# Score rows in paired PSUM banks, and input squares summed on VectorE, in a one-core hybrid decoder layer

## The chip, the core and the metric

The kernel runs on one core of a Trainium2 chip. TensorE (PE) multiplies matrices from SBUF into PSUM, which has eight banks of 512 fp32 columns on 128 partitions. VectorE (DVE) and ScalarE (ACT) read PSUM and SBUF, GpSimd (POOL) works on SBUF, and SyncE (SP) issues the DMAs. The metric is device time in microseconds (us); less is better.

## The reference, cut to what matters

One decoder layer over 1024 tokens of width 1024, all in fp32:

```python
u = rmsnorm(h, g_mix)                       # mean of squares over the 1024 features of a token
z = u @ w_in                                # 1440 columns: x_rnn, x_gate, c_q, c_kv, k_rope
y_rnn = rglru_group(x_rnn, x_gate, ...)     # causal conv, two gates, linear recurrence, gelu
q  = rmsnorm(c_q) @ w_q_up; kv = rmsnorm(c_kv) @ w_kv_up     # 8 heads, 96 columns of q and k
s  = (q . k) * scale, causal                # blocks of 128 queries
p  = softmax(s)                             # row maximum, exponential, row sum
y_att = p @ v
h = h + concat(rmsnorm(y_rnn), rmsnorm(y_att)) @ w_out
h = h + (silu(v @ w_gate) * (v @ w_up)) @ w_down             # v = rmsnorm(h); 2816 wide
h = h + sigmoid(rmsnorm(h) @ w_ple_gate) * rmsnorm(p_in @ w_ple_proj)
return rmsnorm(h, g_final)
```

## The kernel before

The layout is transposed: features on partitions, the 1024 tokens along the free dimension. Each fp32 operand is split into a high and a low part on ACT (`x_h`) and DVE (`x_l`), so that one product is three matmuls (high-high, high-low, low-high) of 128 x 128 by 512 columns.

No instruction is issued where the program text calls it. The calls are recorded, and `Plan.order` lays them out by a list scheduler: each engine takes, of the operations whose inputs are ready by the plan's own estimates, the one with the smallest key. The key is the operation's number in program order, plus an offset for some tiles (`OFF`). An operation whose output tile is in a pool (`bank`: the eight PSUM banks; `slot`: 51 SBUF tiles) can start only when the pool has a free one, and for banks one stays reserved while any bank called for earlier in program order has not been given out (`RES`). The engines then run their lists in that fixed order, and semaphores guard every dependency. Line 361 is the one line that issues everything, so every row below says L361 and is known by its tile names.

The stages that matter here:

- **Input.** For each of eight blocks `k` of the input, `xr` and a weight `w` (`w1`) arrive by DMA, are split, and PE runs 12 matmuls into four banks (`g1`: c_kv and k_rope, shown as `g_a`, `g_b`). `sq_acc` squares the block on ACT, and POOL adds it to `x_acc`. From `x_acc` the `rstd` steps make 1/rms: PE transposes (`nx_ms`), DVE sums (`n_ss`), ACT takes the root (`n_rt`), DVE refines (`n_r`, `n_t`), PE transposes back (`nx_bc`), ACT copies to `nx_rb`. Meanwhile PE runs `in_mm(0)` and `in_mm(1)` (tiles `wn_a`, `wn_b`, 48 matmuls each). `evac` multiplies each bank by its half of `nx_rb` on DVE, and that frees it. DVE also builds the rotary angles (`ang`, `turns`) in this time.
- **Projections and recurrence.** Eight more `in_mm` tiles, with the recurrence on ACT, DVE and POOL.
- **Attention.** For each of 8 heads and 8 query blocks `qb`, `scores` multiplies into one bank (up to 512 keys) or two (`qb` 4 to 7), takes a negated maximum per bank (`nm`), where there are two banks the smaller of the two (a 128 x 1 operation), then one exponential per bank with its row sum read out. `tav_steps` transposes the blocks (`tp`), splits them (`pt`, in part over `pf` on POOL) and multiplies by v (`av`).
- **Output projection, FFN, gate.** FFN products take three banks each (`ff_z`, `ff_y`, `ff_x`); a bank is read by DVE or ACT after each block of matmuls (12 matmuls for gate and up, 6 to 9 for down), and `ff_z` goes on accumulating after it was read.

Of the kernel before, what the change touches and what calls it, by code (L numbers as in the profile page):

```python
# [122 lines left out]
class Buf:  # L123
    def __init__(self, pool, shape, dt, name, tag, bufs):
        self.args, self.tag, self.cap, self.name = (pool, shape, dt), tag, bufs, name
        self.real, self.log, self.left, self.placed = None, [], 0, False


class Op:
# [12 lines left out]
class Plan:  # L142


    def __init__(self, nc):
        self.nc, self.ops, self.tags, self.hold = nc, [], {}, None
        self.engines = {n: getattr(nc, n) for n in ("vector", "scalar", "gpsimd", "tensor", "sync")}

    def tile(self, pool, shape, dt, name, tag, bufs):
# [18 lines left out]
    def cost(self, eng, fn, a, k, out):  # L168
        w = out.width() if isinstance(out, View) else 0
        if fn == "dma_start":  # L170
            v = k["out"] if isinstance(k["out"], View) else k["in_"]
            return v.shape[0] * v.width() * 4 / 360e3, 2.1
        if eng == "tensor":
            if fn == "transpose":
                return 0.108, 0.18
            return w * 0.000417 + 0.0135, 0.18
        if eng == "vector":
            if fn == "reciprocal":
                return 0.065 + w * 0.0063, 0.13
            if fn in ("tensor_reduce", "reduce_sum"):  # L180
                return 0.065 + k["in_"].width() * 0.00104, 0.13
            ptr = 0.061 * any(isinstance(x, View) for x in (k.get("scalar"), *a[2:])) if fn == "scalar_tensor_tensor" else 0.0
            one = fn in ("tensor_copy", "tensor_scalar", "tensor_scalar_mul", "tensor_scalar_add", "tensor_scalar_max")
            if one and all(v.buf.tag != "bank" for v in [*a, *k.values()] if isinstance(v, View)):
                return 0.068 + w * 0.00052, 0.13
            return 0.068 + ptr + w * 0.00104, 0.13
        if eng == "scalar":
            src = k["in_"] if "in_" in k else a[1]
            c = (0.052 if src.buf.tag == "bank" else 0.093) + w * 0.000833
            c += 0.093 * sum(isinstance(k.get(n), View) for n in ("scale", "bias", "accum_out"))  # L190
            return c, 0.14
        return 0.15 + w * (0.0033 if fn == "tensor_copy" else 0.0022), 0.14

# [9 lines left out]
    def add(self, eng, fn, a, k):  # L203
        o = Op()
        o.eng, o.fn, o.a, o.k, o.idx = eng, fn, a, k, len(self.ops)
        o.succ, o.npred, o.ready = [], 0, 0.0
        out = k["out"] if "out" in k else a[0]
        outs = [v for v in (out, k.get("accum_out")) if isinstance(v, View)]
        rest = list(a[1:] if "out" not in k else a) + [v for n, v in k.items() if n not in ("out", "accum_out")]
        ins = [v for v in rest if isinstance(v, View)]  # L210
        o.cost, o.lat = self.cost(eng, fn, a, k, out)
        o.port = self.shares(eng, fn, [v for v in ins if v.width() > 8])
        f = k.get("func") or next((x for x in a if isinstance(x, AF)), None)
        o.table = f.name if eng == "scalar" and f is not None and f.name in FIRST else None
        preds = {self.hold: True} if self.hold else {}
        for v, w in [(v, False) for v in ins] + [(v, True) for v in outs]:
            p0, p1, c0, c1 = v.region
            keep = []
            for (q, r, qw) in v.buf.log:
                hit = r[0] < p1 and p0 < r[1] and r[2] < c1 and c0 < r[3]  # L220
                if hit and (w or qw) and q is not o:
                    preds[q] = True
                if not (w and q is not o and p0 <= r[0] and r[1] <= p1 and c0 <= r[2] and r[3] <= c1):
                    keep.append((q, r, qw))
            keep.append((o, v.region, w))
            v.buf.log = keep
        o.key = o.idx + OFF.get(eng[0] + out.buf.name.rstrip('_ab') if isinstance(out, View) else '', 0) + (DEF if eng in ('vector', 'scalar') and not any(v.buf.tag == 'bank' for v in ins + outs) else 0)
        o.bufs = list(dict.fromkeys(v.buf for v in ins + outs))
        for b in o.bufs:
            if not b.left:  # L230
                b.first = o.idx
            b.left += 1
        for q in preds:
            q.succ.append(o)
            o.npred += 1
        self.ops.append(o)
        return o

    def order(self):
# [14 lines left out]
        table = ""  # L254
        port = 0.0
        frees = []
        for o in self.ops:
            if not o.npred:
                heapq.heappush(avail[o.eng], (o.key, o.idx, o))
# [7 lines left out]

        while left:
            while frees and frees[0][0] <= t:
                _, _, tag, n = heapq.heappop(frees)  # L270
                free[tag] += n
            moved = False
            for e in names:
                while future[e] and future[e][0][0] <= t:
# [6 lines left out]
                while avail[e] and tries < 40:  # L281
                    i, _, o = heapq.heappop(avail[e])
                    tries += 1
                    ok = all(b.placed or free[b.tag] > min(unplaced(b), RES.get(b.tag, 99)) for b in o.bufs)
                    if ok:
                        key = i
                        if e == "scalar" and o.table and o.table not in SAME.get(table, ()):
# [25 lines left out]
                for b in o.bufs:  # L313
                    if b.placed:
                        continue
                    b.placed = True
                    free[b.tag] -= 1
                    q, d = queue[b.tag], ahead[b.tag]
                    d[b.pos] = True
                    while head[b.tag] < len(q) and d[head[b.tag]]:  # L320
# [6 lines left out]
                for b in o.bufs:  # L327
                    b.left -= 1
                    b.done = max(getattr(b, "done", 0.0), o.end)
                    if not b.left:  # L330
                        heapq.heappush(frees, (b.done, b.pos, b.tag, 1))
                for s in o.succ:
                    s.npred -= 1
                    r = start + c + (LAT[e, s.eng] if (e, s.eng) in LAT else o.lat)
# [17 lines left out]
    def emit(self):  # L352
        for o in self.order():
            for b in o.bufs:
                if b.real is not None:
                    continue
                pool, shape, dt = b.args
                b.real = pool.tile(shape, dt, name=b.name, tag=b.tag, bufs=b.cap)
            a = [x.real() if isinstance(x, View) else x for x in o.a]
            k = {n: x.real() if isinstance(x, View) else x for n, x in o.k.items()}  # L360
# [4 lines left out]
DEF = 0  # L365
FG = ((0, 1), (2, 3), (4, 5), (6, 7))
TK = 5
VA = ()
VS = ()
X0 = 0  # L370
SWITCH = 150
RES = {'bank': 1, 'slot': 99}
# [3 lines left out]
def hybrid_layer(ctx, tc, xT, pT, pos, vec, const, const2, w1, wn, wrg, wq, wkv, wo, wg, wu, *rest):  # L376
# [18 lines left out]

    def bank(name):
        return plan.tile(psp, [P, HB], F32, name, "bank", 8)

    def small(shape, name, bufs=2, dt=F32):
        return plan.tile(sml, shape, dt, name, name, bufs)  # L400
# [104 lines left out]

    INVF, ALPHA, BETA, GAMMA = (ccol(i) for i in range(4))

    def sq_acc(acc, src, first, eng, dve=False):
        t = acc if first else slot("sq")
        if dve:  # L510
            V.tensor_mul(t, src, src)
        else:
            A.activation(t, src, AF.Square)
        if not first:
            eng.tensor_add(acc, acc, t)

# [98 lines left out]
        tabs.extend((sc, cse, cpos, cneg))  # L615


    g1 = [pair("g1") for _ in range(2)]
    acc = slot("x_acc")
    xs = []  # L620
    for k in range(8):
# [22 lines left out]
            tb = tables()  # L644
            next(tb)
        xs.append(x2)
        sq_acc(acc, xr, k == 0, V if k in VA else G, k in VS)
        for i in range(2):
            c = slice(i * P, (i + 1) * P)
            mm(g1[i], wh[:, c], wl[:, c], x2, k == 0, k == 7)  # L650
# [6 lines left out]

    def in_mm(i, mid=None):
        wh, wl = weight(("wn", i), 2 if i < 9 else 0)
        pss = pair("wn")  # L660
        for k in range(8):
            c = slice(k * P, (k + 1) * P)
            mm(pss, wh[:, c], wl[:, c], xs[k], k == 0, k == 7)
            if mid and k == 3:
                mid()
        return pss

    def evac(pss, dst):
        for h in range(2):
            V.tensor_mul(dst[:, HS[h]], pss[h], rxs[0][:, HS[h]])  # L670

    cq0p = in_mm(0, lambda: next(nx))

# [5 lines left out]


    ckv = slot("ckv")
    evac(g1[0], ckv)
    krz = slot("krz")
    evac(g1[1], krz)
    cq = [slot("cq0"), slot("cq1")]
    evac(cq0p, cq[0])
    evac(in_mm(1), cq[1])
# [174 lines left out]
    def scores(hd, qb):  # L862
        if qb == 0:
            pA, pA3 = slot("pA"), slot("pA3")
            st[hd] = {"p": {0: pA[:, 0:128], 1: pA[:, 128:384], 2: pA[:, 384:768], 3: pA3[:, 0:512]},
                      "rs": small([P, 2, 8], "rs"), "nm": small([P, 8, 2], "nm")}
        if qb >= 4:
            st[hd]["p"][qb] = slot("pB")
        pd, rs, nm = st[hd]["p"][qb], st[hd]["rs"], st[hd]["nm"]
        (qh, ql), (kh, kl) = qs[hd], ks[hd]  # L870
        n = (qb + 1) * P
        cc = slice(qb * P, (qb + 1) * P)
        chunks = [(c0, min(c0 + HB, n)) for c0 in range(0, n, HB)]
        pss = []
        for i, (c0, c1) in enumerate(chunks):
            w = c1 - c0
            ps = bank("s")
            pss.append(ps)
            T.matmul(ps[:, :w], lhsT=qh[:, cc], rhs=kh[:, c0:c1], start=True, stop=False)
            T.matmul(ps[:, :w], lhsT=qh[:, cc], rhs=kl[:, c0:c1], start=False, stop=False)  # L880
            if c1 == n:
                T.matmul(ps[:, w - P:w], lhsT=ib, rhs=mb, start=False, stop=False)
            T.matmul(ps[:, :w], lhsT=ql[:, cc], rhs=kh[:, c0:c1], start=False, stop=True)
            V.tensor_reduce(out=nm[:, qb, i:i + 1], in_=ps[:, :w], axis=AX.X, op=ALU.max, negate=True)
        if len(chunks) == 2:
            V.tensor_tensor(out=nm[:, qb, 0:1], in0=nm[:, qb, 0:1], in1=nm[:, qb, 1:2], op=ALU.min)
        for i, (c0, c1) in enumerate(chunks):
            A.activation(pd[:, c0:c1], pss[i][:, :c1 - c0], AF.Exp, bias=nm[:, qb, 0:1], accum_out=rs[:, i, qb:qb + 1])

    def tav_steps(hd, hf):  # L890
        q0, nk = 4 * hf, 4 * hf + 4
# [28 lines left out]
        def fin():  # L920
# [6 lines left out]
            V.tensor_add(dst[main, HS[hf]], av[0][main], dst[main, HS[hf]])  # L927
            if hf:
                rs = st[hd]["rs"]
                V.tensor_add(rs[:, 0, 4:8], rs[:, 0, 4:8], rs[:, 1, 4:8])  # L930
                V.reciprocal(ris[-1][:, :, 1 - hd % 2], rs[:, 0])

        def go(i):
            if i < nk:
# [557 lines left out]
```

## Time and profile before

| | us |
|---|---|
| median of 3 runs (1241.95 to 1246.2) | 1243.89 |
| the profiled execution | 1246.8 |
| its span, first to last instruction | 1245.0 |
| PE busy | 1178.9 (95%) |
| DVE busy | 1016.7 (82%) |
| ACT busy | 653.1 (52%) |
| POOL busy | 335.2 (27%) |

The granted TensorE clock was 0.981 of full speed on the mean. A busy PE is not PE at its peak: a matmul of 512 columns is recorded with some 0.39 us (mean 390 ns over 528 of `ff_z`), though in an unbroken row one follows the other sooner.

### The profile page before, as it was taken

What the parts mean: (1) busy time and instruction counts of PE and PEld (TensorE: products, weight loads), DVE (VectorE), ACT (ScalarE), POOL (GpSimd) and SP (SyncE); (2) the same over time, 40 slices, a digit from 0 to 9 for tenths busy, and PEclk for the clock granted to TensorE, in tenths of its full rate; (3) what the DMA queues carried; (4) which work ended last, traced back from release to release, by engine and by line L of the source; (5) the groups of instructions that cost most, each with busy time, mean ns of one, the idle gap of its engine ahead of it and who ended that gap; (6) DMA issues with size and microseconds to landing.
All of it is one profiled execution on the core that took longest, in us unless ns stands there. A gap on an engine that the chain in (4) does not pass through costs nothing.

```text
span 1245.0 us, 15659 instructions
## 1 busy us (share of the span) xinstructions
PE 1178.9 (95%) x5608; PEld 972.0 (78%) x5608; DVE 1016.7 (82%) x1564; ACT 653.1 (52%) x1154; POOL 335.2 (27%) x204
## 2 busy tenths in 40 slices
PE   5999999988989999999999999999699999999995
PEld 4788886866768878888888888888478787888894
DVE  7878797887896989988988888867678676985998
ACT  8338767866774655544444444435222222566565
POOL 6002133564550423331233321233000000244042
PEclk8899999999999999999999999999799999999998
DMA  8100100000031531434344343465997666032352
GB/s 299 47 2 33 51 1 1 2 1 1 34 118 34 204 132 38 167 142 164 119 153 186 128 160 143 162 212 184 378 412 263 239 238 245 27 106 81 117 189 102
DMA packets 50271, 165.36 MB, mean 133 GB/s; under 512 B 5649, under 2 KB 8977, under 8 KB 50193
## 3 DMA queue, kind: packets, MB, share of 16 engines
q1 hardware_dynamic: 50192, 164.37, 36.0%
q8 instruction: 44, 0.72, 0.2%
q14 instruction: 35, 0.28, 0.1%
HBM read 115.58 MB, written 48.76 MB: 132 GB/s over the span
## 4 chain that ended last, share of the span: by engine, by line
PE 71%; DVE 11%; issue 7%; ACT 6%; DMA 3%; POOL 2%; SPq 0%; DVEq 0%; POOLq 0%; ACTq 0%
PE ff_z L361 27%; PE ff_y L361 13%; PE ff_x L361 6%; PE s L361 3%; PE wo_a L361 3%; PE wo_b L361 3%; PE wn_b L361 3%; PE wn_a L361 2%; PE av L361 2%; PE tp L361 2%; DMA wd_r<-in_wd 1%; PE qps L361 1%; DVE nm L361 1%; POOL h L361 1%; DVE pt L361 1%
## 5 line engine op out<-in xcount | busy, mean ns | idle before, releaser
L361 POOL TENSOR_TENSOR silu<-silu,nf_rb 128x512 f32<-128x512 f32 x77 | 120.0, 1584 | 279.6 <-DVE silu L361 258.0
L361 PE MATMUL ff_z<-hx,wd 128*128 128x512 f32 x528 | 129.6, 393 | 11.2 <-DVE h L361 8.7
L361 PE MATMUL ff_z<-x,wg 128*128 128x512 f32 x528 | 128.2, 390 | 0.5 <-DVE x L361 0.5
L361 PE MATMUL ff_z<-x,wu 128*128 128x512 f32 x528 | 127.0, 389 | 0.0
L361 PEld LDWEIGHTS ff_z<-hx,wd 128*128 128x128 f32 x528 | 99.6, 190 | 34.6 <-DVE h L361 9.9
L361 PEld LDWEIGHTS ff_z<-x,wg 128*128 128x128 f32 x528 | 98.9, 188 | 21.5 <-DVE x L361 0.9
L361 PEld LDWEIGHTS ff_z<-x,wu 128*128 128x128 f32 x528 | 99.1, 188 | 20.6
L361 POOL TENSOR_TENSOR p_acc<-p_acc,sq 128x1024 f32<-128x1024 f32 x7 | 19.8, 2825 | 232.9 <-ACT sq L361 232.6
L361 POOL TENSOR_TENSOR pt<-pf,pt 128x512 fp32r<-128x512 f32 (+1 forms) x48 | 58.9, 1233 | 66.5 <-DVE pt L361 27.7
L361 ACT ACTIVATE wd<-wd_r 128x384 fp32r<-128x384 f32 (+1 forms) x64 | 29.9, 492 | 76.5 <-DMA wd_r<-in_wd 30.2
L361 DVE TENSOR_TENSOR h<-ff_z,h 128x512 f32<-128x512 f32 x64 | 43.9, 687 | 29.8 <-PE ff_z L361 21.4
L361 PE MATMUL ff_y<-hx,wd 128*128 128x512 f32 x264 | 66.5, 395 | 0.1
L361 PE MATMUL ff_y<-x,wg 128*128 128x512 f32 x264 | 64.1, 390 | 0.6 <-ACT x L361 0.6
L361 PE MATMUL ff_y<-x,wu 128*128 128x512 f32 x264 | 63.4, 389 | 0.0
L361 PE MATMUL plg<-hg_h,wpg_l 128*128 128x256 f32 (+1 forms) x192 | 61.1, 319 | 1.3 <-DVE wpg_l L361 1.2
L361 PE MATMUL plg<-hg_h,wpg_h 128*128 128x256 f32 (+1 forms) x192 | 61.5, 320 | 0.0
L361 PE MATMUL plg<-hg_l,wpg_h 128*128 128x256 f32 (+1 forms) x192 | 61.2, 319 | 0.0
L361 ACT ACTIVATE wd<-wd_s 128x384 fp32r<-128x384 f32 (+1 forms) x48 | 23.8, 497 | 69.4 <-DVE wd_s L361 47.9
L361 PEld LDWEIGHTS ff_y<-hx,wd 128*128 128x128 f32 x264 | 50.3, 191 | 11.2 <-issue 0.7
L361 PEld LDWEIGHTS ff_y<-x,wg 128*128 128x128 f32 x264 | 49.5, 188 | 11.4 <-ACT x L361 1.0
L361 PEld LDWEIGHTS ff_y<-x,wu 128*128 128x128 f32 x264 | 49.6, 188 | 10.3
L361 PE MATMUL av<-pt,v 128*128 128x512 f32 (+1 forms) x192 | 51.5, 367 | 5.1 <-DVE pt L361 3.3
(391 smaller groups left out, 3219.4 us busy)
## 6 DMA issues: line engine op xcount, KB each, us to landing
hx<-hx SPq DMA_DIRECT2D x154, 512.0 KB, 3.7
wpg_raw<-in_wpg SPq DMA_DIRECT2D x24, 512.0 KB, 3.5
wg_r<-in_wg SPq DMA_DIRECT2D x22, 512.0 KB, 4.9
wu_r<-in_wu SPq DMA_DIRECT2D x22, 512.0 KB, 4.1
wd_r<-in_wd SPq DMA_DIRECT2D x24, 384.0 KB, 6.8
wn_raw<-in_wn SPq DMA_DIRECT2D x10, 512.0 KB, 3.5
wo_raw<-in_wo SPq DMA_DIRECT2D x8, 512.0 KB, 3.7
h<-in_xT SPq DMA_DIRECT2D x8, 512.0 KB, 4.2
```

What stands on the lines that cost most here:

```text
L361: getattr(self.engines[o.eng], o.fn)(*a, **k)
```

## The change

PSUM is now four tiles of two neighbouring banks each, made once (`banks0` to `banks3`). The plan gives every PSUM tile a seat: a tile wider than 512 columns takes two units and needs both banks of one pair free at once; a tile of one unit takes a free bank whose neighbour is in use, and else the free bank of the lowest number. Until now the plan only counted free banks.

Wide tiles are used for the scores of `qb` 4 to 7 (one maximum and one exponential over up to 1024 columns; the smaller-of-two and the adding of two row sums go), for `g1`, and for `in_mm` (one `evac` instruction in place of two). The pairs of the FFN, of the output projection and of the recurrence stay single banks.

The input's `sq_acc` now adds on DVE instead of POOL, and square and add get a key 40 higher (`XLATE`). The plan's estimate of an ACT operation with a row sum grows from 0.093 to 0.2 us for the sum.

```diff
+        self.units, self.at = (2 if tag == "bank" and shape[1] > 512 else 1), None
...
-            c += 0.093 * sum(isinstance(k.get(n), View) for n in ("scale", "bias", "accum_out"))
+            c += 0.093 * sum(isinstance(k.get(n), View) for n in ("scale", "bias"))
+            c += 0.2 * isinstance(k.get("accum_out"), View)
...
-        o.key = o.idx + OFF.get(...) + ...
+        o.key = o.idx + self.shift + OFF.get(...) + ...
...
+        def seat(b):
+            if b.units == 2:
+                return next((i for i in range(0, len(banks), 2) if banks[i] and banks[i + 1]), None)
+            alone = [i for i, f in enumerate(banks) if f and not banks[i ^ 1]]
+            return alone[0] if alone else next((i for i, f in enumerate(banks) if f), None)
...
-                    ok = all(b.placed or free[b.tag] > min(unplaced(b), RES.get(b.tag, 99)) for b in o.bufs)
+                    ok = all(b.placed or free[b.tag] - b.units >= min(unplaced(b), RES.get(b.tag, 99))
+                             and (b.tag != "bank" or seat(b) is not None) for b in o.bufs)
...
+                if b.tag == "bank":
+                    if b.at // 2 not in self.pairs:
+                        n = f"banks{b.at // 2}"
+                        self.pairs[b.at // 2] = pool.tile([P, 2 * HB], F32, name=n, tag=n, bufs=1)
+                    c = b.at % 2 * HB
+                    b.real = self.pairs[b.at // 2][:, c:c + b.units * HB]
+                    continue
...
+    def wide(name):
+        return plan.tile(psp, [P, S], F32, name, "bank", 8)
...
-    g1 = [pair("g1") for _ in range(2)]
+    g1w = [wide("g1") for _ in range(2)]
+    g1 = [[w[:, HS[0]], w[:, HS[1]]] for w in g1w]
...
-        sq_acc(acc, xr, k == 0, V if k in VA else G, k in VS)     # VA and VS are empty
+        plan.shift = XLATE
+        sq_acc(acc, xr, k == 0, V)
+        plan.shift = 0
...
-    def evac(pss, dst):
-        for h in range(2):
-            V.tensor_mul(dst[:, HS[h]], pss[h], rxs[0][:, HS[h]])
+    def evac(ps, dst):
+        V.tensor_mul(dst, ps, rxs[0])
...
-        for i, (c0, c1) in enumerate(chunks):
-            ps = bank("s")
+        ps = wide("s") if n > HB else bank("s")
...
-            V.tensor_reduce(out=nm[:, qb, i:i + 1], in_=ps[:, :w], axis=AX.X, op=ALU.max, negate=True)
-        if len(chunks) == 2:
-            V.tensor_tensor(out=nm[:, qb, 0:1], in0=nm[:, qb, 0:1], in1=nm[:, qb, 1:2], op=ALU.min)
-        for i, (c0, c1) in enumerate(chunks):
-            A.activation(pd[:, c0:c1], pss[i][:, :c1 - c0], AF.Exp, bias=nm[:, qb, 0:1], accum_out=rs[:, i, qb:qb + 1])
+        V.tensor_reduce(out=nm[:, qb:qb + 1], in_=ps[:, :n], axis=AX.X, op=ALU.max, negate=True)
+        A.activation(pd[:, :n], ps[:, :n], AF.Exp, bias=nm[:, qb:qb + 1], accum_out=rs[:, qb:qb + 1])
...
-                V.tensor_add(rs[:, 0, 4:8], rs[:, 0, 4:8], rs[:, 1, 4:8])
-                V.reciprocal(ris[-1][:, :, 1 - hd % 2], rs[:, 0])
+                V.reciprocal(ris[-1][:, :, 1 - hd % 2], rs)
```

## Rows read from the trace of the kernel before

**Rows 1.** Busy time by stage: window and its length, PE, PEld, DVE, ACT, POOL, clock.

```profile
0.00:32.20 32.20, 18.40 (x58) 14.06 (x58) 24.75 (x15) 24.98 (x31) 19.76 (x12) 0.88 0.81 301
...
105.00:181.60 76.60, 76.49 (x338) 62.74 (x336) 66.74 (x69) 57.99 (x71) 20.14 (x8) 1.00 0.08 28
181.60:375.00 193.40, 175.73 (x1016) 140.39 (x1016) 159.21 (x314) 138.61 (x349) 93.32 (x70) 0.99 0.07 25
...
465.00:880.00 415.00, 415.00 (x1840) 343.80 (x1839) 350.90 (x489) 195.16 (x341) 120.05 (x77) 1.00 0.42 155
880.00:1107.00 227.00, 211.26 (x908) 171.81 (x907) 169.28 (x296) 69.68 (x127) 13.21 (x5) 0.96 0.66 245
```

**Rows 2.** Groups, 0 to 66 us: count, busy us, mean ns, idle before, its releaser.

```profile
L361 POOL TENSOR_TENSOR x_acc<-x_acc,sq 128x1024 f32<-128x1024 f32 x7 | 18.7, 2672 | 11.1 <-ACT sq L361 10.7
L361 DVE SCALAR_TENSOR_TENSOR x_l<-xr,vc,x_h 128x1024 fp32r<-128x1024 f32 x7 | 15.9, 2276 | 0.0
L361 DVE TENSOR_TENSOR w_l<-w_raw,w_h 128x256 fp32r<-128x256 f32 x8 | 11.9, 1516 | 4.0 <-ACT w_h L361 4.0
...
L361 PE MATMUL g_a<-x_l,w_h 128*128 128x512 f32 x16 | 8.3, 516 | 8.3 <-DVE x_l L361 8.3
```

**Rows 3.** Input stage in order of time: start, length, instruction, idle before it.

```profile
23.08 1.13 ACT L361 ACTIVATE x_h<-xr,vc 128x1024 fp32r<-128x1024 f32 x1
...
32.09 0.41 DVE L361 TENSOR_TENSOR w_l<-w_raw,w_h 128x256 fp32r<-128x256 f32 x1
...
32.43 1.27 DVE L361 SCALAR_TENSOR_TENSOR x_l<-xr,vc,x_h 128x1024 fp32r<-128x1024 f32 x1
...
37.22 0.68 DVE L361 TENSOR_SCALAR turns<-ang 128x1024 f32<-128x1024 f32 x1
...
45.30 1.21 DVE L361 SCALAR_TENSOR_TENSOR ang<-turns,ang 128x1024 f32<-128x1024 f32 x1
...
53.02 0.69 DVE L361 TENSOR_REDUCE n_ss<-nx_ms 128x4 f32<-128x512 f32 x1 [0.93 <-PE nx_ms L361]
```

**Rows 4.** The chain that ended last, three pieces: start, us, what, matmuls.

```profile
33.45 0.43 PE g_a L361
...
63.23 5.75 PE wn_b L361 x24
...
503.67 2.72 PE ff_z L361 x12
```

**Rows 5.** Groups in attention, 181.6 to 375 us, columns as in Rows 2.

```profile
L361 DVE TENSOR_REDUCE nm<-s 128x1 f32<-128x512 f32 x48 | 32.4, 680 | 1.6 <-PE s L361 1.5
...
L361 ACT ACTIVATE pB<-s,nm 128x512 f32<-128x512 f32 x40 | 27.4, 686 | 21.0 <-DVE nm L361 20.9
...
L361 ACT ACTIVATION_READ_ACCUMULATOR pB<-s,nm 128x1 f32 x64 | 12.8, 200 | 0.0
L361 DVE TENSOR_TENSOR nm<-nm 128x1 f32<-128x1 f32 x32 | 12.0, 374 | 0.3
...
L361 DVE TENSOR_REDUCE nm<-s 128x1 f32<-128x128 f32 x16 | 4.4, 278 | 1.7 <-PE s L361 1.5
...
L361 DVE TENSOR_TENSOR rs<-rs 128x4 f32<-128x4 f32 x8 | 3.1, 393 | 3.0 <-ACT pB L361 3.0
...
L361 ACT ACTIVATE pB<-s,nm 128x128 f32<-128x128 f32 x8 | 2.9, 362 | 0.0
```

**Rows 6.** Two operations in order of time in attention, columns as in Rows 3.

```profile
255.29 2.29 DVE L361 TENSOR_TENSOR nm<-nm 128x1 f32<-128x1 f32 x1
...
255.19 4.72 POOL L361 TENSOR_TENSOR rg_h<-rg_h,nr_rb 128x1024 f32<-128x1024 f32 x2
```

**Rows 7.** FFN, gate-up and then down, in order of time, columns as in Rows 3.

```profile
642.42 0.69 DVE L361 TENSOR_TENSOR ff_u<-ff_y,ff_u 128x512 f32<-128x512 f32 x1 [0.73 <-PE ff_y L361]
...
915.34 1.52 PE L361 MATMUL ff_y<-hx,wd 128*128 128x512 f32 x6
...
918.87 0.68 DVE L361 TENSOR_TENSOR h<-ff_y,h 128x512 f32<-128x512 f32 x1
```

More of the change, by code (lines that the diff above doesn't have):

```diff
@@ L145, in __init__ @@
     def __init__(self, nc):
-        self.nc, self.ops, self.tags, self.hold = nc, [], {}, None
+        self.nc, self.ops, self.tags, self.hold, self.pairs, self.shift = nc, [], {}, None, {}, 0
         self.engines = {n: getattr(nc, n) for n in ("vector", "scalar", "gpsimd", "tensor", "sync")}
@@ L226, in add @@
             v.buf.log = keep
-        o.key = o.idx + OFF.get(eng[0] + out.buf.name.rstrip('_ab') if isinstance(out, View) else '', 0) + (DEF if eng in ('vector', 'scalar') and not any(v.buf.tag == 'bank' for v in ins + outs) else 0)
+        o.key = o.idx + self.shift + OFF.get(eng[0] + out.buf.name.rstrip('_ab') if isinstance(out, View) else '', 0) + (DEF if eng in ('vector', 'scalar') and not any(v.buf.tag == 'bank' for v in ins + outs) else 0)
         o.bufs = list(dict.fromkeys(v.buf for v in ins + outs))
@@ L256, in order @@
         frees = []
+        banks = [True] * free.get("bank", 0)
+        def seat(b):
[3 more added lines that the diff above has]
+            return alone[0] if alone else next((i for i, f in enumerate(banks) if f), None)
         for o in self.ops:
@@ L269, in order @@
             while frees and frees[0][0] <= t:
-                _, _, tag, n = heapq.heappop(frees)
-                free[tag] += n
+                _, _, tag, b = heapq.heappop(frees)
+                free[tag] += b.units
+                if tag == "bank":
+                    banks[b.at:b.at + b.units] = [True] * b.units
             moved = False
@@ L316, in order @@
                     b.placed = True
-                    free[b.tag] -= 1
+                    free[b.tag] -= b.units
+                    if b.tag == "bank":
+                        b.at = seat(b)
+                        banks[b.at:b.at + b.units] = [False] * b.units
                     q, d = queue[b.tag], ahead[b.tag]
@@ L330, in order @@
                     if not b.left:
-                        heapq.heappush(frees, (b.done, b.pos, b.tag, 1))
+                        heapq.heappush(frees, (b.done, b.pos, b.tag, b))
                 for s in o.succ:
@@ L357, in emit @@
                 pool, shape, dt = b.args
+                if b.tag == "bank":
+                    if b.at // 2 not in self.pairs:
[4 more added lines that the diff above has]
+                    continue
                 b.real = pool.tile(shape, dt, name=b.name, tag=b.tag, bufs=b.cap)
@@ L367 @@
 TK = 5
-VA = ()
-VS = ()
+XLATE = 40
 X0 = 0
@@ L506, in hybrid_layer, with sq_acc @@
     INVF, ALPHA, BETA, GAMMA = (ccol(i) for i in range(4))
-    def sq_acc(acc, src, first, eng, dve=False):
+    def sq_acc(acc, src, first, eng):
         t = acc if first else slot("sq")
[L510 to L513, printed above, removed]
+        A.activation(t, src, AF.Square)
         if not first:
@@ L659, in in_mm @@
         wh, wl = weight(("wn", i), 2 if i < 9 else 0)
-        pss = pair("wn")
+        ps = wide("wn")
+        pss = [ps[:, HS[0]], ps[:, HS[1]]]
         for k in range(8):
@@ L665, in in_mm @@
                 mid()
-        return pss
-    def evac(pss, dst):
-        for h in range(2):
-            V.tensor_mul(dst[:, HS[h]], pss[h], rxs[0][:, HS[h]])
+        return ps
+    def evac(ps, dst):
+        V.tensor_mul(dst, ps, rxs[0])
     cq0p = in_mm(0, lambda: next(nx))
@@ L681, in hybrid_layer @@
     ckv = slot("ckv")
-    evac(g1[0], ckv)
+    evac(g1w[0], ckv)
     krz = slot("krz")
-    evac(g1[1], krz)
+    evac(g1w[1], krz)
     cq = [slot("cq0"), slot("cq1")]
@@ L865, in scores @@
             st[hd] = {"p": {0: pA[:, 0:128], 1: pA[:, 128:384], 2: pA[:, 384:768], 3: pA3[:, 0:512]},
-                      "rs": small([P, 2, 8], "rs"), "nm": small([P, 8, 2], "nm")}
+                      "rs": small([P, 8], "rs"), "nm": small([P, 8], "nm")}
         if qb >= 4:
@@ L872, in scores @@
         cc = slice(qb * P, (qb + 1) * P)
-        chunks = [(c0, min(c0 + HB, n)) for c0 in range(0, n, HB)]
-        pss = []
-        for i, (c0, c1) in enumerate(chunks):
-            w = c1 - c0
-            ps = bank("s")
-            pss.append(ps)
-            T.matmul(ps[:, :w], lhsT=qh[:, cc], rhs=kh[:, c0:c1], start=True, stop=False)
-            T.matmul(ps[:, :w], lhsT=qh[:, cc], rhs=kl[:, c0:c1], start=False, stop=False)
-            if c1 == n:
-                T.matmul(ps[:, w - P:w], lhsT=ib, rhs=mb, start=False, stop=False)
-            T.matmul(ps[:, :w], lhsT=ql[:, cc], rhs=kh[:, c0:c1], start=False, stop=True)
-            V.tensor_reduce(out=nm[:, qb, i:i + 1], in_=ps[:, :w], axis=AX.X, op=ALU.max, negate=True)
-        if len(chunks) == 2:
-            V.tensor_tensor(out=nm[:, qb, 0:1], in0=nm[:, qb, 0:1], in1=nm[:, qb, 1:2], op=ALU.min)
-        for i, (c0, c1) in enumerate(chunks):
-            A.activation(pd[:, c0:c1], pss[i][:, :c1 - c0], AF.Exp, bias=nm[:, qb, 0:1], accum_out=rs[:, i, qb:qb + 1])
+        ps = wide("s") if n > HB else bank("s")
+        for c0 in range(0, n, HB):
+            c1 = min(c0 + HB, n)
+            T.matmul(ps[:, c0:c1], lhsT=qh[:, cc], rhs=kh[:, c0:c1], start=True, stop=False)
+            T.matmul(ps[:, c0:c1], lhsT=qh[:, cc], rhs=kl[:, c0:c1], start=False, stop=False)
+            if c1 == n:
+                T.matmul(ps[:, n - P:n], lhsT=ib, rhs=mb, start=False, stop=False)
+            T.matmul(ps[:, c0:c1], lhsT=ql[:, cc], rhs=kh[:, c0:c1], start=False, stop=True)
+        V.tensor_reduce(out=nm[:, qb:qb + 1], in_=ps[:, :n], axis=AX.X, op=ALU.max, negate=True)
+        A.activation(pd[:, :n], ps[:, :n], AF.Exp, bias=nm[:, qb:qb + 1], accum_out=rs[:, qb:qb + 1])
     def tav_steps(hd, hf):
```

## The prediction, on record before the result

> **What bounds the kernel now.** I read the page first (PE 95% busy, DVE 82%), then the busy time by stage, because an average over stages with different limits says little here. From 105 to 181.6 us and from 465 to 880 us PE is busy all the time [rows 1]; nothing that this change does to DVE or ACT can shorten those. Two stages are different. In the first 32.2 us PE is busy for 18.4. In attention, 181.6 to 375 us, PE is busy for 175.7 of 193.4 us, so at least 17.7 us stand open, beside 159.2 us of DVE and 138.6 of ACT [rows 1]. No engine is full there: the three wait for one another.
>
> Next I looked at what PE waits for in the input stage. It is DVE: 8.3 us of idle time ahead of the matmuls on `x_l` [rows 2]. And DVE is slow there, not short of data: the seven full splits `x_l` took 2.28 us on the mean, yet one taken after POOL's last add took 1.27; `w_l` took 1.52 on the mean and 0.41 then [rows 2, 3]. POOL's seven adds to `x_acc` ran in just that time, 18.7 us of them [rows 2]. So a DVE instruction with two SBUF inputs stands still while POOL adds. By these rows the adds cost DVE 7 x (2.28 - 1.27) + 8 x (1.52 - 0.41) = 7.1 + 8.9 = 16 us. The last high part was begun on ACT at 23.08, so the last `x_l` could have come at about 25.5 us; yet at 32.43 DVE began a split that still had two behind it.
>
> The Trainium skill, "SBUF — State Buffer", section "Who interferes with whom", names this: VectorE and GpSimd share a read interface, and the one that starts second is held for the other's whole instruction. The trace agrees (a mean of 2.28 us beside the adds, 1.27 without).
>
> **The change in the input stage.** Removed: 7 POOL adds, and with them 16 us of standing still on DVE. Added: 7 adds on DVE of 1024 fp32 pairs, for which the nearest row is a DVE operation of that width, 1.21 us [rows 3], together 8.5 us. Their keys are 40 higher, about two input blocks, so the splits go first, and on ACT the squares give way to `x_h`.
>
> PE then is fed faster than it works. Twelve matmuls in an unbroken row take 2.72 us, 0.227 each; at the lower of its two clock levels (1.2 GHz), which it shows after an idle stretch, one takes 0.43 [rows 4]. The first stage is 8 x 12 = 96 matmuls, 21.8 us, and `in_mm(0)` 48, 10.9 us. Starting at 5.5 us (the stage had 18.4 busy us of 32.2 [rows 1]), with 12 x 0.2 = 2.4 us lost to the lower level at first, PE can finish all 144 at about 41 us. Then it meets a new wait. `in_mm(1)` now wants two neighbouring banks at once, while `nx_ms` and `nx_bc`, called for earlier, keep a reserve; with `g1` and `in_mm(0)` holding three pairs, it can't start before `nx_bc` has its banks. Before, half of it (24 matmuls) ran ahead of that point. So the input stage now ends with the norm: what counts is when `nx_rb` is there.
>
> When is that? DVE work that must go before: 8 splits of x (10.3 us), 8 of w (3.3), 7 adds (8.5), ten angle steps, five of 1.2 and five of 0.7 (9.6), two weight splits (2.4) [rows 3]: 34 us from 4 us on, so `x_acc` is done at 38 to 40 us. But before, PE got to its last `nx_ms` only at about 52, behind the late `g1` matmuls, and from the `n_ss` at 53.02 to the first matmul after the norm at 63.23 it took 10.2 us [rows 3, 4]. Now PE is free when the sum is ready: 39, plus 1 for the transposes, plus 10 for the same chain: 50 us. From there PE has 48 matmuls of `in_mm(1)` to do (10.9 us) and, having idled, restarts at the lower level (2.4 us again): done at 63.3. Before, at 63.23, 24 were left [rows 4], and they ended at about 69, 68.7 without their breaks. Gain 5.4 us. Bounds: if the chain sheds the weight splits that were put between its small steps, 45 us, gain 10; if DVE gets the adds last and the norm comes at 58, a loss of 2.6. I take 5, since both halves of the sum are durations of these very instructions. From 105 to 181.6 us PE is full [rows 1], so what is won is kept.
>
> `evac` in one instruction of 1024 columns saves the fixed part of one per tile. The reductions give it: 680 ns at 512 columns and 278 at 128 [rows 5], a slope of 1.05 ns and a fixed 144 ns. Twelve times 0.14 is 1.7 us of DVE beside a full PE: nothing on the path.
>
> **The change in attention.** Thirty-two rows (8 heads, `qb` 4 to 7) change. Removed on DVE: 32 operations `nm<-nm`, 12.0 us; 32 x 0.144 = 4.6 us of fixed parts of maxima; 8 adds `rs<-rs`, 3.1 us, and 3.0 us of waiting before them [rows 5]. Together 19.7 busy us of 159. A 128 x 1 operation should take 0.15, and its mean is 0.374 because it too is held by POOL: the one at 255.29 lasted 2.29 us and stood behind a POOL multiply from 255.19 [rows 6]. Where the next instruction also has two SBUF inputs it will inherit the hold; where it reads PSUM it won't. Removed on ACT: 32 read-outs of 0.2 us (6.4), and 32 fixed parts; 686 ns at 512 and 362 at 128 columns give 254 ns fixed, 8.1 us [rows 5]. Together 14.5 of 138.6 us.
>
> Added: the maximum of the first 512 columns can't start before the second half is multiplied, and the pair is held until the one exponential of up to 1024 columns (254 + 0.845 x 1024 = 1.12 us) ends. Behind the wide maximum (144 + 1.05 x 1024 = 1.22 us) on DVE stand the `pt` splits, for which PE's `av` waits; that is 0.5 us later for them, but the sum of the work ahead is smaller.
>
> What is it worth? If all that DVE loses were on the path, 19.7 us; PE's own open time caps it near 18 (somewhat more, since recorded matmuls overhang). If only the longest holds of `nm<-nm` were on the path, 2 us (the one at 255.29 alone cost that). The idle time that ACT spends ahead of its exponentials on `nm`, 20.9 us [rows 5], says that the chain score, maximum, exponential often ends last, so I go nearer to the upper end: 11 us, some 55% of what DVE sheds.
>
> **The other stages.** Gate and up, 415 us, are full on PE. There DVE waits for the block to end and has read it out 0.7 us later, while the next block lasts 2.72 us [rows 4, 7], so a tighter reuse of banks is hidden. In the down stage blocks last 1.4 to 2 us and reading comes later at times: the `ff_y` group from 915.34 (six matmuls, done about 916.7) is added to `h` only until 919.55 [rows 7]. A bank taken again at once could cost some tenths there, a few times: 1 us in all.
>
> **Sum.** The profiled execution took 1246.8 us, span 1245.0. Minus 5, minus 11, plus 1: 1231.8. It is 2.9 us above the median of the runs, so against 1243.9 the forecast is 1229.
>
> **The rivals.**
>
> *Pairs starve attention.* A wide row needs an aligned free pair, and `tp`, `av` and `qps` leave single holes. For it: a wide tile holds both banks until the exponential ends. Against it: single tiles are seated beside a busy neighbour, so at most one pair is broken most of the time. Then PE gives back what DVE sheds: attention 0 to 3, input 5, about 1240.
>
> *The input stage gives nothing.* The norm is ready only at 55 us (PE's break-even: 55 + 2.5 + 10.9 = 68.4), for DVE is busy with angles first. For it: DVE has 34 us of work by then. Against it: the holds are gone. Time 1246.8 - 11 + 1 - 2.9 = 1234.
>
> *Banks are taken again too soon (slower).* The seat takes the lowest free bank, so a bank just emptied is written again first, where any other free bank would have rested. If read-outs lag the plan by more than one block, PE stops at the next product's first block. In the down stage that would be 16 products with three banks each; at 0.6 us a time 29 us, so the end is near 1229 + 28 = 1257. It decides where the lag passes 1.4 to 2 us; the group at 915.34 shows one of 2.9 us [rows 7]. Against it: in all that stage PE has only 227 - 211 = 16 us open [rows 1], and there `ff_z` already waits for its own read-out.
>
> The Trainium skill speaks for this rival: "Perfetto Trace Analysis", section "Optimizing Tensor Performance", wants independent groups of matmuls to rotate through different banks, so that reading one out overlaps the next group. By that rule the seats cost time wherever the lag is longer than a block; this trace shows such lags in the down stage only.
>
> **How the numbers follow.** The forecast 0.55, the input stage without gain 0.15, starved attention 0.15, banks too soon 0.15. A change of under 0.3% (3.7 us: 1240.2 to 1247.6) can't be told from none. Faster: 0.55 + 0.15 and a third of the starved case, 0.75; same 0.11; slower 0.14. The forecast's own range, from its terms' ends (input 0 to 10, attention 6 to 18), is 1217 to 1238. For 8 in 10 it has to take in the starved case: 1215 to 1245.
>
> **What would show it.** Right: no POOL add below 35 us, `x_l` at 1.27 us throughout, PE without waits on `x_l`, and then one gap of some 8 us ahead of `wn` until `nx_rb`; in attention 64 maxima and 64 exponentials, a DVE of about 140 busy us, and a stage of about 182 us. Wrong: an attention stage still above 190 us with PE waiting for exponentials ahead of `s`, or PE waits on DVE `h` all through the down stage.

## The result: a quarter slower, and the profile after

The changed kernel takes 1557.53 us (median of 4 runs, 1556.47 to 1558.95) against 1244.8 for the kernel before (4 runs): a ratio of 1.2517 [1.249, 1.2544]. The forecast was 1229, faster. Of the runs below, one of the seven of b_one_bank_tiles took 1491 us at a granted clock of 0.748 and is left out of its ratio. The profiled execution has a span of 1557.1 us, 312 more than before.

In the list of busy times (busy us, share of the span, instructions) PE, the engine that bounded the kernel, has fallen from 95 to 82%:

```profile
PE 1274.2 (82%) x5608; PEld 953.9 (61%) x5608; DVE 973.1 (62%) x1487; ACT 647.1 (42%) x1090; POOL 299.2 (19%) x197
```

DVE and ACT were busy for less time than before, as the change meant, and PE executed as many matmuls as before (5608). So PE waited. That its busy time rose all the same, from 1178.9 to 1274.2 us, fits: recorded matmuls overlap in an unbroken row, and a stop shows the end of the last one in full (more on this under i_ffn_zy). The busy time by stage says where (columns as in [rows 1]; the windows are the same stages, at their new places):

```profile
0.00:32.20 32.20, 26.25 (x105) 20.71 (x106) 24.52 (x31) 27.95 (x34) 1.15 (x5) 1.00 0.85 317
194.10:410.70 216.60, 181.65 (x1003) 137.76 (x1002) 140.60 (x239) 133.76 (x284) 88.79 (x70) 0.98 0.06 23
497.70:1075.00 577.30, 466.52 (x1864) 337.10 (x1865) 348.85 (x496) 200.06 (x353) 118.90 (x79) 1.00 0.32 118
1075.00:1392.00 317.00, 240.48 (x916) 168.55 (x916) 167.94 (x295) 69.07 (x126) 12.87 (x5) 0.96 0.47 173
```

The first line is better than its counterpart in [rows 1]: 26.3 busy us of PE in the first 32.2 instead of 18.4. The gate and up products, in which PE never stopped before (415.00 of 415.00), now have 111 open us in 577. From the first score matmul, the last `av`, the first `wg`, the last `wu` and the last `wd` of both traces, the 312 us divide so: up to attention +12.7, attention +25.0 (191.6 to 216.6), output projection +3.8, gate and up +154.6 (422.9 to 577.5), down +89.4 (232.0 to 321.4), the rest +26.6.

So 244 of 312 us lie in the FFN, whose arithmetic, tiles and operations the change left alone. PE's waits there, from 497.7 to 1392 us, but for two more of 3.3 us together (what it waited for: us in total, times, longest), and then the longest sum of the kernel before, from 456 to 1111 us:

```profile
PE banks L384 <- DVE h L384: 72.6, 85, 8.3
PE banks L384 <- DVE silu L384: 42.2, 53, 0.9
PE banks L384 <- DVE ff_u L384: 25.3, 32, 0.9
PE banks L384 <- ACT silu L384: 22.9, 33, 1.2
PE banks L384 <- ACT ff_u L384: 21.0, 30, 0.7
```

```profile
PE ff_z L361 <- DVE h L361: 8.7, 3, 7.6
```

Those are 233 waits, 184 us, nearly all for the read-outs of finished blocks (`ff_u` and `silu` behind gate and up, `h` behind down), where the kernel before has 3 on `h` and none on the others. Three of them in order of time, two with their read-out (start, length, instruction, idle before it):

```profile
698.10 3.28 PE L384 MATMUL banks<-x,wu 128*128 128x512 f32 x13 [0.79 <-DVE ff_u L384]
...
701.41 0.69 DVE L384 TENSOR_TENSOR ff_u<-banks,ff_u 128x512 f32<-128x512 f32 x1 [1.38 <-PE banks L384]
...
702.16 2.60 PE L384 MATMUL banks<-x,wu 128*128 128x512 f32 x10 [0.79 <-DVE ff_u L384]
...
704.60 0.85 PE L384 MATMUL banks<-x,wg 128*128 128x512 f32 x3
705.55 0.69 DVE L384 TENSOR_TENSOR silu<-banks,silu 128x512 f32<-128x512 f32 x1 [1.04 <-PE banks L384]
...
706.30 3.24 PE L384 MATMUL banks<-x,wg 128*128 128x512 f32 x13 [0.85 <-DVE silu L384]
```

PE ends its row of matmuls at 701.38, DVE reads from 701.41 to 702.10, PE goes on at 702.16. The read-out is not late, as a lag of the kind in [rows 7] would be: it begins 0.03 us after the matmuls end. PE stands still for just as long as it lasts, though in the program its next block goes into another bank.

The seats explain which bank. A single tile takes a free bank whose neighbour is in use, so a block of the FFN is seated beside the block that is still to be read out, and these two banks are now halves of one allocated tile. My theory: the wait that guards a tile is kept for the whole tile, so a matmul into one half waits for the read-out of the other. The rival, from the prediction: banks are taken again too soon, in a kernel whose waits are each bank's own.

### The profile page after: what moved, and what is told of

Read it like the earlier page. It is cut to its first block, busy times and chain, and to the rows that moved or that the text cites. A ratio compares the mean times of both kernels' runs of the same rounds, so it can differ in the third digit from the quotient of the medians.

```text
span 1557.1 us, 15479 instructions
## 1 busy us (share of the span) xinstructions
PE 1274.2 (82%) x5608; PEld 953.9 (61%) x5608; DVE 973.1 (62%) x1487; ACT 647.1 (42%) x1090; POOL 299.2 (19%) x197
## 4 chain that ended last, share of the span: by engine, by line
PE 66%; DVE 15%; ACT 8%; issue 8%; DMA 1%; POOL 1%; SPq 0%; DVEq 0%; ACTq 0%; POOLq 0%
PE banks L384 66%; DVE h L384 4%; DVE silu L384 2%; DVE ff_u L384 1%; ACT silu L384 1%; ACT ff_u L384 1%; POOL h L384 1%; ACT pf L384 1%; DVE nm L384 1%; ACT e L384 1%; DVE pt L384 1%; DVE xc L384 1%; DMA h<-hd 0%; ACT L384 0%; ACT pA L384 0%
## 5 line engine op out<-in xcount | busy, mean ns | idle before, releaser
L384 PE MATMUL banks<-hx,wd 128*128 128x512 f32 x924 | 242.9, 410 | 76.5 <-DVE h L384 72.3
L384 PE MATMUL banks<-x,wg 128*128 128x512 f32 x924 | 234.9, 401 | 56.1 <-DVE silu L384 32.8
L384 PE MATMUL banks<-x,wu 128*128 128x512 f32 x924 | 234.1, 401 | 54.9 <-DVE ff_u L384 25.3
L384 PEld LDWEIGHTS banks<-hx,wd 128*128 128x128 f32 x924 | 170.2, 192 | 148.8 <-DVE h L384 107.7
L384 PEld LDWEIGHTS banks<-x,wg 128*128 128x128 f32 x924 | 167.4, 188 | 121.2 <-DVE silu L384 50.3
L384 PEld LDWEIGHTS banks<-x,wu 128*128 128x128 f32 x924 | 167.8, 188 | 119.3 <-DVE ff_u L384 38.9
L384 DVE TENSOR_TENSOR h<-banks,h 128x512 f32<-128x512 f32 x128 | 87.3, 689 | 150.5 <-PE banks L384 142.2
L384 PE MATMUL banks<-hg_h,wpg_l 128*128 128x256 f32 (+1 forms) x192 | 62.0, 324 | 7.0 <-DVE gt L384 4.6
L384 PE MATMUL banks<-hg_h,wpg_h 128*128 128x256 f32 (+1 forms) x192 | 62.1, 324 | 3.4 <-DVE gt L384 1.8
L384 PE MATMUL banks<-hg_l,wpg_h 128*128 128x256 f32 (+1 forms) x192 | 61.5, 321 | 1.3 <-DVE gt L384 1.3
L384 ACT ACTIVATE silu<-banks 128x512 f32<-128x512 f32 x33 | 19.7, 596 | 89.4 <-PE banks L384 89.4
```

The source lines that it names most:

```text
L384: getattr(self.engines[o.eng], o.fn)(*a, **k)
```

## Experiments

The first four ran together, the next three together, the last by itself, each beside runs of the kernel before (medians 1245.32, 1246.89 and 1244.65 us). a, d and i have two runs each, b seven, the others four. Stage lengths, from the same first and last matmuls (us; down from the last `wu` to the last `wd`):

| | span | first `s` | attention | gate, up | down |
|---|---|---|---|---|---|
| before | 1245.0 | 181.4 | 191.6 | 422.9 | 232.0 |
| after | 1557.1 | 194.1 | 216.6 | 577.5 | 321.4 |
| a_pair_tiles | 1618.7 | 212.0 | 254.0 | 577.3 | 324.7 |
| b_one_bank_tiles | 1248.7 | 185.6 | 191.8 | 422.8 | 231.6 |
| c_squares | 1234.0 | 170.7 | 191.0 | 424.1 | 231.2 |
| d_seats_apart | 1274.5 | 189.3 | 209.8 | 423.7 | 230.0 |
| e_own_pair | 1224.1 | 168.6 | 180.7 | 426.5 | 230.7 |
| f_own_pair_scores | 1233.2 | 181.4 | 178.2 | 426.3 | 230.0 |
| g_two_own_pairs | 1238.9 | 170.7 | 190.3 | 424.8 | 232.0 |
| i_ffn_zy | 1385.4 | 168.6 | 190.5 | 512.7 | 293.3 |

**a_pair_tiles and b_one_bank_tiles: the same order and seats, two allocations.** Both are the kernel before, all its operations single, with the change's rule for single seats. They differ in one thing: a cuts the eight banks from four tiles, b allocates eight.

```diff
+            alone = [i for i, f in enumerate(banks) if f and not banks[i ^ 1]]
+            return alone[0] if alone else next((i for i, f in enumerate(banks) if f), None)
...
+                        self.pairs[b.at // 2] = pool.tile([P, 2 * HB], F32, name=n, tag=n, bufs=1)    # a
+                        self.pairs[b.at] = pool.tile([P, HB], F32, name=n, tag=n, bufs=1)             # b
```

> The kernel before, its operations and their order unchanged; only the PSUM banks are given out by the new seats, as halves of four two-bank tiles, and nothing is wide. Theory 1 (sharing: dependencies are kept per two-bank tile, so a matmul into one bank waits for the read-out of its neighbour): the FFN slows as in the changed kernel, where PE waited 0.7 to 0.8 us at each of 7 blocks of 38 products, some 200 us or more; total 1450 to 1560. Theory 2 (the banks are taken again too soon): slow as well, and as slow as the run with eight one-bank tiles. Theory 3 (wide score and projection tiles or the new plan are what costs): about 1244.

> The same order and the same seats as the run with pair tiles, but each bank is a tile of its own. Theory 1 (sharing): no false wait is left, 1244, at most a few us more where a bank is taken again at once. Theory 2 (banks too soon): the seats alone cost, 1450 or more. Theory 3: about 1244 too.

a took 1622.2 us, 1.3028 [1.2992, 1.3063]; b 1250.0, 1.0039 [1.002, 1.0058]. PE's waits in the FFN of a:

```profile
PE banks L379 <- DVE h L379: 73.6, 86, 8.2
PE banks L379 <- DVE silu L379: 42.2, 53, 0.9
PE banks L379 <- DVE ff_u L379: 25.3, 32, 0.9
PE banks L379 <- ACT silu L379: 22.3, 33, 0.7
PE banks L379 <- ACT ff_u L379: 21.0, 30, 0.7
```

They are the changed kernel's, nearly to a wait. In the FFN of b all that is left is this, but for three waits of 0.6 us and less, and in order of time 84 matmuls stand in one unbroken row:

```profile
PE banks L378 <- DVE h L378: 9.2, 3, 8.2
PE banks L378 <- DVE wd L378: 3.4, 1, 3.4
PE banks L378 <- ACT wd L378: 2.8, 2, 1.4
```

```profile
635.42 19.20 PE L378 MATMUL banks<-x,wu 128*128 128x512 f32 x84
```

The shared tile alone makes the loss, 372 us between two kernels with the same instructions in the same order in the same seats, and no wide operation is needed for it. Stage by stage a loses against b 26 us up to attention, 62 in it, 6 in the output projection, 248 in the FFN and 28 behind it. The rival is priced too: taking the lowest bank again costs 5 us, 4 of them ahead of attention (the last `wn` matmul at 178.7 instead of 174.8), none in the FFN. Of the 4 us, 2.4 are two waits on DVE `zg`, the longest 2.1; right behind it the granted clock is 0.53 from 164 to 167.5 us, where a 512-column matmul follows the other after 0.43 us instead of 0.227, an estimated 1.6 us more.

**d_seats_apart: one line of the changed kernel reversed.** A single tile takes a bank whose neighbour is free.

```diff
-            alone = [i for i, f in enumerate(banks) if f and not banks[i ^ 1]]
-            return alone[0] if alone else next((i for i, f in enumerate(banks) if f), None)
+            apart = [i for i, f in enumerate(banks) if f and banks[i ^ 1]]
+            return apart[0] if apart else next((i for i, f in enumerate(banks) if f), None)
```

> The changed kernel with one line turned round: a single bank is taken where its neighbour is free, not where it is in use, so that ff_z, ff_y and ff_x lie in three pairs. Theory 1 (sharing): most FFN waits go, gate and up take about 425 us again, total 1235 to 1300, with what is left where pairs are still shared (attention, and the ends of products). Theory 2 or 3: the FFN stays as slow as in the changed kernel, 1500 or more.

1278.73 us, 1.0269 [1.0235, 1.0303]: 279 of the 313 us are back. The first fence has PE's two longest sums of waits in the FFN, the second those in attention:

```profile
PE banks L384 <- DVE h L384: 8.6, 4, 7.0
PE banks L384 <- DVE wd L384: 3.4, 1, 3.4
```

```profile
PE banks L384 <- ACT pf L384: 6.4, 9, 1.6
PE banks L384 <- DVE ya L384: 5.2, 6, 1.4
```

Three FFN tiles can sit in three pairs, and the 233 waits are gone. In attention, as I read it, more tiles live at once than there are pairs, so some sharing stays; the stage is 18 us longer than before although DVE has less to do. Whether wide rows that find no whole pair free have a part in that, no run separates. That the seats matter at all with the same tiles is again what the theory says: a wait costs something only where two users of one tile take turns.

**i_ffn_zy: the loss put back by hand.** From g (below; no shared tiles in the FFN), the first two of the three FFN blocks become halves of one wide tile; the third keeps its own bank.

```diff
-        z, y, x = (bank("ff_" + n) for n in "zyx")
+        zy = wide("ff_zy")
+        z, y, x = zy[:, HS[0]], zy[:, HS[1]], bank("ff_x")
```

> The kernel with two own two-bank tiles (1239 us) with one edit: in the FFN ff_z and ff_y are the two halves of one such tile, ff_x stays in a bank of its own. Sharing theory, with the price of one wait from the changed kernel (0.69 to 0.79 us, the read-out's own length and its two hand-overs): of the blocks z y z y z x z, four follow a block of the neighbour bank, so 4 x 38 products x 0.75 = 114 us more, 1353 in all, 1330 to 1370; ff_x causes no wait. If instead every block waited for the read-out before it whatever the tile (7 x 38 x 0.75 = 200), 1440; if the tile does not matter, 1239.

1388.66 us, 1.115 [1.1095, 1.1205]: 146.5 us of span more than g, and by the table 149 us more in the FFN. PE's waits for read-outs in the FFN, then PE in order of time, part of a product:

```profile
PE ff_zy L362 <- DVE h L362: 53.9, 62, 8.1
PE ff_zy L362 <- ACT ff_u L362: 24.1, 33, 1.7
PE ff_zy L362 <- ACT silu L362: 22.7, 33, 1.1
PE ff_zy L362 <- DVE ff_u L362: 8.9, 11, 0.9
PE ff_zy L362 <- DVE silu L362: 8.7, 11, 0.9
```


```profile
702.87 3.48 PE L362 MATMUL ff_zy<-x,wu 128*128 128x512 f32 x14 [0.74 <-ACT ff_u L362]
707.04 2.79 PE L362 MATMUL ff_zy<-x,wu 128*128 128x512 f32 x11 [0.69 <-ACT ff_u L362]
710.52 2.56 PE L362 MATMUL ff_zy<-x,wu 128*128 128x512 f32 x10 [0.69 <-ACT ff_u L362]
713.86 2.83 PE L362 MATMUL ff_zy<-x,wu 128*128 128x512 f32 x11 [0.78 <-DVE ff_u L362]
716.53 2.88 PE L362 MATMUL ff_x<-x,wu 128*128 128x512 f32 x12
719.25 2.88 PE L362 MATMUL ff_zy<-x,wu 128*128 128x512 f32 x12
```

A product has seven blocks. Where one half of the shared tile follows the other PE stops, four times a product; ahead of `ff_x`, and ahead of the `ff_zy` block behind it, it does not. The count was as expected: 22 products of gate and up with 4 waits are 88, which is what the list has, and 16 of down are 64, where it has 62. `ff_x` waits for no read-out. The price was not as expected, and the time is above the 1330 to 1370: 146.5 to 149 us by 152 is 0.96 to 0.98 us a wait, where the rows show 0.7 to 0.8 of idle time. The recorded end of a matmul overhangs the next one's start: 0.39 us is recorded, 0.227 is the pace [rows 4], and a stop lets the last 0.16 show. That makes some 0.9; what is left I did not trace. In the changed kernel 38 x 7 = 266 blocks end, 233 waits are listed, and the FFN lost 244 us, 1.05 for each wait.

**c_squares and f_own_pair_scores: each half of the change without shared tiles.** c is the kernel before with the squares added on DVE, 40 keys later. f is the kernel before with the wide score rows, one PSUM tile of two banks of its own and six of one bank; besides the wide rows the two-bank tile serves half of `g1` and every second output of the output projection.

```diff
+        plan.shift = 40                                   # c
+        sq_acc(acc, xr, k == 0, V)
+        plan.shift = 0
...
+        return plan.tile(psp, [P, S], F32, name, "wide", 1)     # f; "bank" has 6
```

> The kernel before with only the input's squares added on DVE, key 40 higher; all PSUM tiles as before. My step: 16 us of holding on DVE go, 8.5 us of adds come, the sum is ready at about 39 us and half of in_mm(1) still runs ahead; 1234 to 1240, about 5 to 10 us less than before. Rival (the input stage gains nothing, the norm ends it anyway): 1244, with PE idle ahead of nx_bc.

> The kernel before with the wide score rows (one maximum, one exponential, no smaller-of-two, no adding of row sums), the wide tile being a tile of its own of two banks beside six one-bank tiles, so that no single bank has a neighbour in its tile; g1 uses the wide tile once, the output projection now and then; squares stay on POOL. My step: DVE sheds 19.7 busy us and ACT 14.5 in attention, 11 us off the stage (6 to 18), 1227 to 1239. Rival (with one wide tile at a time the rows queue for it): PE waits for exponentials ahead of s, 1244 or more. Rival (the busy time shed was idle time anyway): 1241 to 1247 with attention at 190 us or more.

c took 1235.17 us, 0.9922 [0.99, 0.9944]; f 1236.52, 0.992 [0.9902, 0.9939]. Groups of c up to 66 us (columns as in [rows 2]), then PE in order of time:

```profile
L361 DVE SCALAR_TENSOR_TENSOR x_l<-xr,vc,x_h 128x1024 fp32r<-128x1024 f32 x7 | 8.9, 1278 | 0.0
L361 DVE TENSOR_TENSOR x_acc<-x_acc,sq 128x1024 f32<-128x1024 f32 x7 | 8.5, 1217 | 0.0
```

```profile
39.80 1.09 PE L361 MATMUL nx_ms<-cs,x_acc 128*128 128x128 f32 x8
...
44.85 0.39 PE L361 MATMUL wn_a<-x_h,wn_l 128*128 128x512 f32 x1
```

`x_l` fell from 2276 [rows 2] to 1278 ns, the adds take 1217, and behind `nx_ms` PE has `wn` matmuls to do while the norm is made: single banks let half of `in_mm(1)` run ahead, so the norm costs PE two waits of 1.2 and 0.7 us in place of a gap, and the stage gives 10 us where I had 5 for the paired version. A part of it is the clock: in the kernel before, PE waited 5.20 us for `x_l` until 19.83 and 3.13 until 32.23, and the granted clock was 0.54 from 17 to 24 us and 0.52 from 31 to 38; in c there is one such wait, of 0.65 us, and the granted clock is 1.00 from 17 to 40 us.

f's attention, by stage and by group:

```profile
181.40:359.60 178.20, 169.98 (x1020) 139.28 (x1019) 149.14 (x249) 132.08 (x288) 92.04 (x70) 1.00 0.08 28
```

```profile
L361 DVE TENSOR_REDUCE nm<-s 128x1 f32<-128x1024 f32 x8 | 9.8, 1222 | 4.6 <-PE s L361 4.6
...
L361 ACT ACTIVATE pB<-s,nm 128x1024 f32<-128x1024 f32 x8 | 8.9, 1115 | 7.3 <-DVE nm L361 7.3
```

Attention falls by 13.4 us. Gate and up then takes 3.4 more than before, at its start: PE waits 1.5 us on ACT `silu` and 1.8 on POOL `f_acc` (the kernel before has two waits there, of 0.6 and 0.5), and from 450 to 456 us the granted clock is 0.76. The wide operations last what the prediction made of the fixed part and the slope (1.22 and 1.12 us).

**e_own_pair and g_two_own_pairs: both halves, without sharing.** e is f with the squares of c and the change's estimate for row sums; its one wide tile also serves four of the ten `in_mm`. g has two wide tiles and four single ones, and all of `g1` is wide.

```diff
-        return plan.tile(psp, [P, HB], F32, name, "bank", 8)
+        return plan.tile(psp, [P, HB], F32, name, "bank", 6)      # e; g: 4
+        return plan.tile(psp, [P, S], F32, name, "wide", 1)       # e; g: 2
```

> Both parts of the change without shared tiles: squares on DVE, wide score rows, every second in_mm and one g1 in the one own two-bank tile, six one-bank tiles for the rest. If sharing was the only fault of the change, the two gains add: 10 us of the squares and 11 us of the scores, 1221 to 1228. If the scores gain nothing, 1233 to 1238, as the squares alone.

> As the run with one own two-bank tile, but two of them and four one-bank tiles: wide rows no longer queue for one tile, singles are fewer. If the wait for the wide tile is what limits attention, faster than with one; if the singles tp, av and qps limit it, slower, by 5 to 15 us.

e took 1227.83 us (1225.84 to 1228.65), 0.985 [0.9831, 0.9869], and beats both kernels; g 1238.98, 0.9936 [0.9913, 0.9958]. Attention and gate and up of e, by stage:

```profile
168.60:349.30 180.70, 171.19 (x1017) 140.42 (x1016) 149.60 (x250) 132.28 (x288) 91.74 (x70) 0.99 0.08 27
432.90:859.30 426.40, 423.08 (x1866) 349.77 (x1865) 358.93 (x496) 200.93 (x351) 124.68 (x79) 1.00 0.43 154
```

The halves add up: c gave 10.2 us and f 10.4, together 20.6, and e gave 19.1. g starts attention when c does, and then loses 10 us of e's gain in attention (190.3 against 180.7); it differs from e there in having four single banks and two wide tiles instead of six and one.

## Why the prediction was wrong, point by point

- **The step that failed** is "a tighter reuse of banks is hidden", with "1 us in all" for the other stages. It took for granted that each bank has its own wait, as it had while each was its own tile. The diff showed the opposite: `pool.tile([P, 2 * HB]...)` once, and halves cut from it. The FFN paid 244 us, and the other stages 68, net of what the change won there; a against b, where nothing is won, has 248 and 122.
- **The rival "banks are taken again too soon"** named the place and the sign (PE stopping on DVE `h` all through the down stage), and its test came true. Its mechanism and price did not: as it was priced it decides where a read-out lags by more than a block, and would have cost 28 us; b shows 5 us for it, none in the FFN. What stopped PE needs no lag: any read-out holds up the neighbour's next matmul for its whole length. The rule of the Trainium skill quoted there ("Perfetto Trace Analysis", "Optimizing Tensor Performance") was kept to by the letter, since groups did rotate through banks; the overlap it promises came in b, with 422.8 us of gate and up, and did not in a, with 577.3. In this kernel rotating helps only between banks that are separate tiles.
- **The input stage** was right. In the changed kernel no POOL add runs in it, `x_l` and `w_l` are freed from the hold, and the adds cost 8.5 us:

```profile
L384 DVE SCALAR_TENSOR_TENSOR x_l<-xr,vc,x_h 128x1024 fp32r<-128x1024 f32 x7 | 8.9, 1275 | 0.0
L384 DVE TENSOR_TENSOR x_acc<-x_acc,sq 128x1024 f32<-128x1024 f32 x7 | 8.5, 1212 | 0.0
...
L384 DVE TENSOR_TENSOR w_l<-w_raw,w_h 128x256 fp32r<-128x256 f32 x8 | 3.2, 417 | 4.1 <-ACT w_h L384 4.1
```

In order of time PE there has the forecast gap between the transposes of the sum and `wn`, in three pieces around the transposes of the norm:

```profile
39.66 1.09 PE L384 MATMUL banks<-cs,x_acc 128*128 128x128 f32 x8
...
49.00 1.75 PE L384 MATMUL banks<-cs,n_r 128*128 128x128 f32 x7 [6.63 <-DVE n_r L384]
...
52.60 1.22 PE L384 MATMUL banks<-x_h,wn_h 128*128 128x512 f32 x2 [0.69 <-ACT nx_rb L384]
```

The sum was forecast for 38 to 40 us, the first matmul behind the norm for 50, the gap for 8; they came at 39.7, 52.6 and with 8.0 (6.63, 0.69 and 0.69). PE then ended `in_mm(1)` at 65.6 us where the forecast had 63.3, some 3 us earlier than before instead of 5. That was lost again before attention began, 12.7 us later than before. By the runs this is the shared tiles: a, on shared tiles without the input part, is later still (212.0), b on single ones is 4 us later than before (185.6).
- **Attention** was right in its operations and wrong in this kernel. DVE fell to 140.6 busy us, forecast 140; the stage grew to 216.6, forecast 182. Without sharing the time holds: 178.2 in f, 180.7 in e. Of the range 6 to 18 for that gain, f measures 13.4, the term was 11. That 140.6 hit the forecast is luck, though: in f, whose stage is as short as forecast, DVE is busy for 149.1 us. The operations that were to go went there: 64 maxima take 47.1 us, where maxima, `nm<-nm` and `rs<-rs` took 66.1. But DVE's busy time shows only 9 of those 19 us. A part of the difference is that their records overlapped those of others, and that work on `v` moved into the stage (4.9 us, 2.2 before); the rest I did not trace.
- **"Pairs starve attention"**: not what decided the time, since the FFN has no wide tile. Whether it adds to the 25 us that attention lost, beside sharing (62 us there between a and b), no run separates. A shortage shows in g, 10 us, as I read it of single banks.
- **The time** of 1229 was the time of a change that shares no tiles: e takes 1227.83. That is 19.1 us less than the kernel before beside it, where the prediction had 15, so that the times agree to 1 us is in part luck.

## What to carry to other kernels

When several buffers become slices of one allocation, price every one of their hand-overs anew: a writer of one slice may wait for the readers of the others, and a seat rule that packs users together makes that the usual case. Give what must be read as one piece an allocation of its own, and leave the rest single. And where an unbroken row of matmuls is what bounds a kernel, count its block ends first: here 233 stops of about 1 us cost 244 us, where the two parts of the change could win 20.

## What the runs showed that I had not expected

- A stop of PE between two blocks costs more than its idle time in the trace: 0.7 to 0.8 us recorded, 0.96 to 0.98 us measured in i.
- The stops of 0.7 to 0.8 us in gate and up did not lower the clock: the granted clock there is 1.00 in the changed kernel, as in [rows 1]. In down it is 0.96 in both. Ahead of attention it fell: it was 0.50, the lower of its two levels, from 166 to 176 us, a few matmuls behind a wait of PE of 2.57 us on DVE `k_l` that ended at 165.0; the kernel before has 1.00 from 105 to 181.6 [rows 1].
- Freeing DVE of POOL's adds was worth as much as the whole of the wide score rows: 10.2 and 10.4 us, and the two nearly add up.
